# S5 layer with FFN on one Trainium2 core: context scaling and eigenvalue powers on VectorE, accumulating transfers ahead of the pair products

## The chip, the cores and the metric

The kernel runs on one core of a Trainium2 chip, in one launch. The metric is the device time of that launch in microseconds (us); the median of three runs is compared. The core's engines run side by side, each through its own instructions in order, and meet through semaphores: TensorE (PE in the profile, PEld for its weight loads), VectorE (DVE), ScalarE (ACT), GpSimd (POOL) and SyncE (SP), which here only issues transfers. Transfers (DMA) are issued from the queues of SyncE, ScalarE and GpSimd; the ones that add onto their destination are issued from GpSimd.

## The reference

One layer (depth 1) of a hybrid backbone with a bidirectional S5 mixer, over 1024 latent tokens and 256 context tokens of width 1024, all in float32. Cut to what matters here:

```python
def s5_direction(u_ctx, u_lat, lam_re, lam_im, log_step, b_re, b_im, c_re, c_im):
    lam = lax.complex(lam_re, lam_im)
    lam_bar = jnp.exp(lam * jnp.exp(log_step)[:, None])
    b_bar = ((lam_bar - 1.0) / lam)[..., None] * lax.complex(b_re, b_im)
    c_mat = lax.complex(c_re, c_im)
    def run(u, h0):
        bu = jnp.einsum('lgh,gnh->lgn', u, b_bar)
        bu = bu.at[0].add(lam_bar * h0)
        a = jnp.broadcast_to(lam_bar, bu.shape)
        _, h = lax.associative_scan(_linear_combine, (a, bu), axis=0)
        return jnp.einsum('lgn,ghn->lgh', h, c_mat).real, h[-1]
    y_c, h_c = run(u_ctx, jnp.zeros(lam_bar.shape, lam_bar.dtype))
    y_l, _ = run(u_lat, h_c)
    return y_c, y_l

h_l = modulate(rms_norm(x, norm_mix), m_l[0], m_l[1])      # latent tokens, scale and shift from silu(c)
h_c = modulate(rms_norm(ctx, norm_mix), m_c[0], m_c[1])    # context tokens, from silu(c_ctx)
y_c, y_l = s5_mixer(h_c, h_l, ...)                         # both directions, then d_skip, GELU and a GLU
x = x + m_l[2] * y_l
x = x + m_l[5] * swiglu(modulate(rms_norm(x, norm_ffn), m_l[3], m_l[4]), w1, w3, w2)
return rms_norm(x, norm_final)
```

There are 64 groups of 16 channels with 64 complex states each. The context's final state starts the latent scan; the output is the latent stream.

## The kernel before, in words

Eight consecutive tokens form a chunk, so there are 32 context chunks and 128 latent ones. `U` (128 partitions: 8 tokens by 16 channels) holds, for each of the 64 groups, 160 columns: `Xc` the first 32 (context), `X` the other 128 (latent). A *block* `b` is eight groups; there are 8 blocks, and 16 steps `hb` go through 8 blocks by 2 directions. `bd(hb)` gives block and direction: from step 4 on, block `hb // 2` and direction `hb % 2`.

The kernel first computes the eigenvalues' exponentials on VectorE (to about 28 us), then runs the loop over `hb` (L698 to L755), then a scan over chunks on VectorE (`scan`, L839), beside which GpSimd, TensorE and ScalarE work through a written-out list (`PROG1`), and after it `PROG2`, the GLU and the FFN.

What the loop does for one step, and on which engine:

- `sums(hb)`: TensorE multiplies the block's columns of `U` by the weights `Win`, and ScalarE copies the results into the state arrays `STQ` (L590 for direction 0, L592 and L593 for direction 1). Two PSUM buffers `pv` turn, and ScalarE frees them.
- `bl_make(n)`: two products of 128x1024 that make the weights of step `n`, into the buffers `bls(n)`: on GpSimd for the steps in `PMUL` (6, 8, 10, 13 among them), on VectorE for the others (7, 9, 11, 12, 14, 15).
- `bl_sum(n)`: the sum of the two products. For `n` of 4 to 15 it is an accumulating transfer of 512 KB, issued from GpSimd's queue (L433); for `n` above 15 it does nothing.
- `bl_tr(n)`: TensorE transposes the summed weights, ScalarE copies them to `Win` (L446) and copies one more piece (`bb_copy`, L451).
- `pair(n)`: four products and sums of 128x256 that combine neighbouring latent chunks of step `n`, on GpSimd for the steps in `PPAIR` (3, 5, 7, 8, 9, 11, 12, 13, 15), else on VectorE. `ctx_tree` does the like for the context chunks, on VectorE.
- the latent inputs are scaled by the row statistics (`rs_lat`, VectorE) and then by the modulation (`u_act`, ScalarE, L497). The context inputs of block `b` are scaled by `u_ctx(b)`: one product and one sum over 128x256 on GpSimd, with the columns `cols`, which `mix_cols` copies from PSUM to SBUF. `UCTX` (L685) puts blocks 4, 5, 6 and 7 at steps 6, 7, 9 and 11.
- `pw_mul` makes powers of the eigenvalues: four products and sums on GpSimd, called once in step 3 (one power, 128x128 and 128x64 elements) and twice in step 4 (two powers, then one).
- `power8`, `powers` and `pw_full` prepare further powers; `mix_scale`, `mix_sel` and `mix_cols` turn the modulation rows into columns, for groups 0 to 31 ahead of the loop and for 32 to 63 in step 4.

Within a step the order of the source sets each engine's order: `sums(hb)`, `bl_tr(hb+2)`, `rs_lat`, `u_act`, `u_ctx`, `pair(hb-1)`, `ctx_tree`, `bl_sum(hb+5)`, `bl_make(hb+6)`, `pw_mul`. So in step 9 GpSimd has `u_ctx(6)`, `pair(8)` and then the issue of transfer 14; in step 10 `pair(9)` and then the issue of transfer 15.

From step 9 SyncE's queue holds the load of the C columns (`cs_load(0)`, L651), whose buffer is the one that transfer 13 reads, and then, from step 10, the 256 KB loads of the modulation weights (`ada_load`, L520), which write over buffers of the loop. ScalarE changes the sign of part of the C columns in step 11 (`cs_sign(0)`, L655).

The vector engines' elementwise operations all go through the helper `tt` (L77), so lines of the profile are told apart by tiles: `ru` is `U`, `ra` holds the states and the powers, `lta`, `ltb`, `lbt`, `tq` are PSUM banks that VectorE uses for its second operands, `c` and `rxc` hold the weight products, `r` holds `cols` and other small arrays. `colp` are 128 columns of `ltb` that hold modulation columns in PSUM; `u_lat` reads them for blocks 0 and 1 alone.

Of the kernel before, what the change touches and what calls it, by code (L numbers as in the profile page):

```python
# [24 lines left out]
G = 64  # L25
# [17 lines left out]
def s5_ffn_kernel(tc, a, out):  # L43
    nc = tc.nc
    V, S, E, PE, SY = nc.vector, nc.scalar, nc.gpsimd, nc.tensor, nc.sync
    ctx = ExitStack()
    with ctx:
        ctx.enter_context(tc.manual_schedule())
        sb = ctx.enter_context(tc.tile_pool(name="sb", bufs=1))
        def region(tag, kb, dt=F32):  # L50
            return sb.tile([P, int(kb * 256)], dt, tag=tag, name=tag)

        def view(reg, kb, shape, parts=P):
            off = int(round(kb * 256))
            n = int(np.prod(shape))
            v = reg[:parts, off:off + n]
            if len(shape) > 1:
                names = "abcdef"[:len(shape)]
                v = v.rearrange(f"p ({' '.join(names)}) -> p {' '.join(names)}",
                                **{k: d for k, d in zip(names, shape)})  # L60
            return v
# [3 lines left out]
        RA = region("ra", 80.5)  # L65
# [5 lines left out]
        def bc(ap, axis, n):  # L71
            sh = list(ap.shape)
            sh.insert(axis, n)
            return ap.unsqueeze(axis).to_broadcast(sh)

        def tt(o, x, y, op, eng=V):
            eng.tensor_tensor(out=o, in0=x, in1=y, op=op)  # L77
# [10 lines left out]
        MUL, ADD, SUB = OP.mult, OP.add, OP.subtract  # L88
# [10 lines left out]
        ident, blk, sel = (cpk[:, HC + i * P:HC + (i + 1) * P] for i in range(3))  # L99
# [36 lines left out]
        LTb = pA.tile([P, 512], F32, tag="r1", name="ltb")  # L136
        lbt = pA.tile([P, 512], F32, tag="r4", name="lbt")
# [15 lines left out]
        X, Xc = U[:, :, 32:160], U[:, :, 0:32]  # L153
# [41 lines left out]
        def ada1(h, *ks):  # L195
            for k in ks:
                for b in range(2):
                    i = 2 * b + h
                    PE.matmul(prow[32 * i:32 * i + 2], scs[:, k], stage[h][k][:, b], start=k == 0, stop=k == 7, tile_position=(0, 32 * i))
# [79 lines left out]
        rsp, rcp, colp = LTb[:, 256:384], LTb[:, 128:160], LTb[:, 384:512].rearrange("p (b g) -> p b g", b=2)  # L279
# [61 lines left out]
        def pw_mul(o, x, y):  # L341

            m = x.shape[1]
            a_, b_ = (view(RA, kb, [m, 2, G]) for kb in (42, 43))
            yr, yi = (bc(bc(y[:, i], 1, 2), 1, m) for i in range(2))
            tt(a_, x, yr, MUL, E)
            tt(b_, x[:, :, ::-1], yi, MUL, E)
            tt(o[:, :, 0], a_[:, :, 0], b_[:, :, 0], SUB, E)
            tt(o[:, :, 1], a_[:, :, 1], b_[:, :, 1], ADD, E)

        LH = view(RXc, 0, [2, 3, G])
        SQ = [LS[:, 0], view(RXa, 7.25, [3, G]), LH[:, 0], LH[:, 1], LS[:, 1]]
# [1 line left out]
        def power8():  # L354

            pt = pv2()[:, 0, 0:128].rearrange("p (r q d e) -> p r q d e", r=2, q=8, d=2)
            for gp in range(2):
                for d in range(2):
                    sl = slice(64 * d, 64 * d + 64)
                    PE.matmul(pt[64 * gp:64 * gp + 64, :, :, d], ident[:, sl],  # L360
                              PW[:, 7].rearrange("p r (q e t) -> p r q e t", q=8, t=2)[:, :, :, :, gp], start=True, stop=True)
            pt = pt.rearrange("p r q d e -> p r (q d e)")
            S.copy(SQ[0][:, 0::2], pt)
            S.activation(SQ[0][:, 1], pt[:, 1], AF.Copy, scale=-1.0)
            S.copy(LQ[0], SQ[0])
# [36 lines left out]
        def bls(hb):  # L402
            return BL1[hb % 5], BL2[hb % 3]
# [26 lines left out]
        def bl_sum(hb):  # L430

            if 4 <= hb < 16:
                E.dma_start(bls(hb)[0], bls(hb)[1], accum_op=ADD)  # L433
            elif hb < 4:
                tt(bls(hb)[0], bls(hb)[0], bls(hb)[1], ADD, E)

        def bl_tr(hb, copy=True):
            b, d = bd(hb)
            t1 = bls(hb)[0]
            pt, w_ = pv2(), Win[hb % 3]  # L440
            for j in range(2):
                for i in range(4):
                    PE.transpose(pt[:, j, P * i:P * i + P], t1[:, 4 * j + i].rearrange("p s h -> p (s h)"), ident)
            if not copy:
                return pt, w_
            S.copy(w_.rearrange("p j i n -> p (j i n)"), pt.rearrange("p j n -> p (j n)"))  # L446
            bb_copy(hb)
# [5 lines left out]
        r4, mx = view(RA, 74, [4, P]), view(RA, 76, [2, 2, 32])  # L453

        def mix_rows():
            S.copy(r4, prow.rearrange("p (m n) -> p m n", m=4))

        def mix_turn():
            for m in range(4):
                PE.transpose(prow[:, P * m:P * m + P], r4[:, m], ident)  # L460
# [11 lines left out]

        def mix_sel(h):

            PE.matmul(colp[:, :, 32 * h:32 * h + 32], sel, mx[:, 0], start=True, stop=True)
            PE.matmul(pcol, sel, mx, start=True, stop=True)

        def mix_cols(h, eng=V):
# [5 lines left out]

        def u_ctx(b):
            gs = slice(8 * b, 8 * b + 8)
            tt(Xc[:, gs], Xc[:, gs], bc(cols[:, 1, 1, gs], 2, 32), MUL, E)
            tt(Xc[:, gs], Xc[:, gs], bc(cols[:, 1, 0, gs], 2, 32), ADD, E)

# [87 lines left out]
        def sums(hb):  # L577
            b, d = bd(hb)
            for j in range(2):
                w, pv = Win[hb % 3][:, j], pv2()  # L580
                for ri in range(2):
                    for i in range(4):
                        c0 = 160 * (i // 2)
                        PE.matmul(pv[64 * (i % 2):64 * (i % 2) + 64, ri, c0:c0 + 160], w[:, i, 64 * ri:64 * ri + 64],  # L584
                                  U[:, 8 * b + 4 * j + i], start=True, stop=True)
                pv = pv[:, :, 0:320].rearrange("p r (e c) -> p c r e", e=2)
                e = 8 * (b % 2) + 4 * d + 2 * j
                st = STQ[b // 2][:, :, :, e:e + 2]
                if d == 0:
                    S.copy(st, pv)  # L590
                else:
                    S.copy(st[:, 159:31:-1], pv[:, 32:160])  # L592
                    S.copy(st[:, 31::-1], pv[:, 0:32])  # L593
# [104 lines left out]
        for hb in range(16):  # L698
            sums(hb)
            ada1(1, *ADA1.get(hb, ()))  # L700
            if hb == 0:
                power8()
            if hb == 3:
                mix_rows()
            for n in BLTR.get(hb, (hb + 2,)):
                if n < 16:
                    bl_tr(n)
            if hb == 3:
                mix_turn()
            if hb == 4:  # L710
                mix_scale(1)
                mix_sel(1)
            if hb in RSL:
                rs_lat(RSL[hb])
            if hb == 4:
                mix_cols(1)
                tq = pA.tile([P, 512], F32, tag="r3", name="tq")
                LQ += [t[:, o_:o_ + 192].rearrange("p (r e) -> p r e", e=G) for t, o_ in ((tq, 0), (tq, 192), (LTb, 256))]
            if hb == 0:
                tt(Xc[:, 16:], ctxT[:, 16:], bc(rcp, 1, G - 16), MUL)  # L720
            if hb == 1:
                powers(0)
            if hb == 2:
                powers(1)
                SY.dma_start(BXY[:, 1], a["bxy"][:, 3])
            if hb in UACT:
                u_act(*UACT[hb])
            if hb in UCTX:
                u_ctx(UCTX[hb])
            if hb >= 1:  # L730
                pair(hb - 1, E if hb - 1 in PPAIR else V)
            if hb == 5:
                powers(2, 3)
            for a_ in CTREE.get(hb, ()):
                ctx_tree(*a_)
            if hb + 6 in (7, 9, 11, 12, 14, 15):
                lb_psum(hb + 6)
            bl_sum(hb + 5)
            bl_make(hb + 6)
            if hb == 3:  # L740
                pw_mul(PW[:, 2:3], PW[:, 0:1], PW[:, 1])
                tt(KD.rearrange("p q g h -> p (q g) h"), bc(pat, 1, 8), bc(dcol, 2, HC), MUL, E)
            if hb == 4:
                pw_mul(PW[:, 4:6], PW[:, 0:2], PW[:, 3])
                pw_mul(PW[:, 6:7], PW[:, 2:3], PW[:, 3])
            if hb in (6, 8):
                pw_full(hb // 2 - 3)
            if hb == 9:
                cs_load(0)
            if hb == 11:  # L750
                V.tensor_copy(LQ[4], SQ[4])
                cs_sign(0)
            for _ in range(CLAT.get(hb, 0)):
                CL0.pop(0)()
            ada_load(ADA2.get(hb, 0))  # L755
# [752 lines left out]
        for f in list(PAIRS) + [NFT - 2]:  # L1508
# [6 lines left out]
            if f in PAIRS:  # L1515
                U = [("U", f + 1, j) for j in range(7)]
                n = 4 if f == NPL else 1
# [172 lines left out]
        for i, (kind, ft, j) in enumerate(seq):  # L1690
# [12 lines left out]
            if kind == "U":  # L1703
# [4 lines left out]
                if (ft, j) in LAST:  # L1708
                    k, h = LAST[ft, j]
# [63 lines left out]
```

## Time and profile before

| what | us |
|---|---|
| median of 3 runs | 1023.65 |
| lowest and highest run | 1022.72, 1023.95 |
| the profiled execution's own time | 1024.33 |
| its span, first to last instruction | 1022.5 |
| TensorE busy in the span | 962.6 (94%) |
| VectorE busy | 785.6 (77%) |
| GpSimd busy | 762.7 (75%) |
| ScalarE busy | 438.5 (43%) |
| mean granted TensorE clock | 0.987 |

The span begins with the first instruction and all times of rows are counted from there. A row of the timeline has start and duration in us, engine, line, operation, output tile from input tiles, shape and count, and in brackets the idle time ahead of it with what ended it; rows of like instructions in a row are merged. In rows of waits, the engine and line on the left waited for the one on the right: total us, number of times, longest. Rows of DMA issues give the size and the us from issue to landing.

### The profile page before, as it was taken

The numbers are of one execution on the slowest core, as the hardware profiler recorded it, in microseconds if no ns is written. First come the engines' busy times: TensorE is split into PE (matmuls) and PEld (weight loads), VectorE is DVE, ScalarE is ACT, GpSimd is POOL, SyncE is SP. The second block draws the span as 40 slices with busy tenths as digits, with TensorE's granted clock in tenths as the row PEclk, the third lists the DMA queues.
The fourth block names the chain that finished last, engine by engine and source line by source line (L and its number), as shares of the span: only waits on it lengthen the run. The fifth ranks groups of instructions, "written<-read, shape, count | busy, mean of one in ns | idle before, by whom it ended". The sixth has DMA issues, their size and how long they took to land. (4 is left out here: it accounts for less than half of the span.)

```text
span 1022.5 us, 18552 instructions
## 1 busy us (share of the span) xinstructions
PE 962.6 (94%) x6988; PEld 774.2 (76%) x6988; DVE 785.6 (77%) x1642; ACT 438.5 (43%) x858; POOL 762.7 (75%) x590
## 2 busy tenths in 40 slices
PE   5987798868999999999999999999999999999996
PEld 1466523658999988778888888888888888888885
DVE  7989799994365778788968768585958778686977
ACT  5477622324353663533334343424333343324337
POOL 5799999991591457879686877778686877777664
PEclk9999999998999999999999999999999999999998
DMA  9765997222622021011212011121212111121205
GB/s 318 292 132 96 276 350 243 91 73 57 235 80 86 2 104 62 21 42 42 83 41 73 32 52 61 43 73 52 73 42 81 41 40 56 45 70 52 72 21 165
DMA packets 48546, 98.96 MB, mean 97 GB/s; under 512 B 4284, under 2 KB 18876, under 8 KB 47176
## 3 DMA queue, kind: packets, MB, share of 16 engines
q1 hardware_dynamic: 43272, 86.64, 25.3%
q0 software_dynamic: 2016, 7.34, 3.8%
q10 hardware_dynamic: 3168, 3.79, 1.1%
q8 instruction: 55, 0.90, 0.4%
q14 instruction: 35, 0.29, 0.1%
HBM read 84.25 MB, written 6.17 MB: 88 GB/s over the span
## 5 line engine op out<-in xcount | busy, mean ns | idle before, releaser
L77 POOL TENSOR_TENSOR c<-rxc,c 128x512 fp32r<-128x512 f32 x128 | 166.6, 1316 | 53.5 <-ACT c L1227 52.7
L1287 PE MATMUL ut<-ra,c 128*128 128x512 f32 x400 | 155.7, 389 | 1.2 <-DVE ra L77 1.2
L1286 PE MATMUL ut<-ra,c 128*128 128x512 f32 x400 | 155.7, 389 | 0.2 <-ACT ra L1227 0.2
L1288 PE MATMUL ut<-ra,c 128*128 128x512 f32 x400 | 155.6, 389 | 0.0
L1227 ACT CAST c<-rxc 128x512 fp32r<-128x512 f32 x128 | 79.1, 622 | 146.8 <-PE xt L1581 53.3
L1581 PE MATMUL xt<-c,c 128*128 128x512 f32 x540 | 129.7, 389 | 0.0
L1581 PEld LDWEIGHTS xt<-c,c 128*128 128x128 f32 x540 | 101.4, 188 | 21.0
L77 DVE TENSOR_TENSOR ru<-ru,xt 128x1024 f32<-128x1024 f32 x90 | 106.8, 1213 | 8.6 <-PE xt L1581 6.6
L77 DVE TENSOR_TENSOR ru<-ut,ru 128x512 f32<-128x512 f32 x98 | 67.1, 686 | 43.1 <-PE ut L1288 37.7
L1287 PEld LDWEIGHTS ut<-ra,c 128*128 128x128 f32 x400 | 75.1, 188 | 17.1 <-POOL rxc L77 1.5
L1286 PEld LDWEIGHTS ut<-ra,c 128*128 128x128 f32 x400 | 75.1, 188 | 16.1 <-ACT ra L1227 0.6
L1288 PEld LDWEIGHTS ut<-ra,c 128*128 128x128 f32 x400 | 75.1, 188 | 15.5
L77 POOL TENSOR_TENSOR c<-rw,c 128x512 fp32r<-128x512 f32 (+1 forms) x29 | 42.5, 1465 | 38.8 <-ACT c L1227 38.2
L1286 PE MATMUL ut<-c,c 128*128 128x512 f32 x160 | 62.3, 389 | 0.8 <-DVE rxa L77 0.8
L77 POOL TENSOR_TENSOR c<-ru,c 128x512 fp32r<-128x512 f32 (+1 forms) x39 | 55.5, 1422 | 10.1 <-ACT c L1227 5.7
L77 POOL TENSOR_TENSOR rxc<-rxc 128x512 f32<-128x512 f32 x40 | 61.5, 1536 | 1.6
L1288 PE MATMUL ut<-c,c 128*128 128x512 f32 x160 | 62.3, 389 | 0.0
L1287 PE MATMUL ut<-c,c 128*128 128x512 f32 x160 | 62.3, 389 | 0.0
L1581 PE MATMUL ut<-c,c 128*128 128x512 f32 x216 | 51.9, 389 | 0.0
L584 PE MATMUL pv<-ru,c 128*64 128x160 f32 x512 | 43.7, 312 | 7.3 <-POOL ru L77 2.6
L77 DVE TENSOR_TENSOR pe<-pe,ru 128x256 f32<-128x256 f32 x64 | 27.4, 428 | 29.5 <-ACT pe L1127 17.4
L77 DVE TENSOR_TENSOR ru<-ru,ut 128x512 f32<-128x512 f32 x76 | 47.2, 678 | 0.7 <-ACT ru L1635 0.5
(449 smaller groups left out, 2576.0 us busy)
## 6 DMA issues: line engine op xcount, KB each, us to landing
c<-in_ada_w SPq DMA_DIRECT2D x46, 256.0 KB
rxc<-in_w SPq DMA_DIRECT2D x38, 256.0 KB
rxc<-in_w SPq DMA_DIRECT2D x19, 512.0 KB
ru<-in_w SPq DMA_DIRECT2D x11, 512.0 KB
rw<-in_w SPq DMA_DIRECT2D x11, 512.0 KB
ra<-in_ada_w SPq DMA_DIRECT2D x10, 512.0 KB
ra<-in_ada_w SPq DMA_DIRECT2D x18, 256.0 KB
ru<-in_xT SPq DMA_DIRECT2D x4, 1024.0 KB
```

The lines of the kernel that those rows point to most:

```text
L77: eng.tensor_tensor(out=o, in0=x, in1=y, op=op)
L584: PE.matmul(pv[64 * (i % 2):64 * (i % 2) + 64, ri, c0:c0 + 160], w[:, i, 64 * ri:64 * ri + 64], U[:, 8 * b + 4 * j + i], start=True, stop= ...
L1227: S.copy(o[0], x)
L1286: PE.matmul(pu, wh, bh, start=start, stop=False)
L1287: PE.matmul(pu, wh, bl, start=False, stop=False)
L1288: PE.matmul(pu, wl, bh, start=False, stop=stop)
L1581: PE.matmul(pd, w[:, cs_], b, start=j in (1, 2, 4) and n == 0, stop=n == 2, skip_group_check=j not in (1, 2, 4))
```

## The change

Three parts, all in the loop and what it calls:

1. `pw_mul` runs on VectorE. It first copies the factor `y` into a PSUM bank (`yc`, in `lbt`), and its two temporaries are a piece of `ltb` (PSUM) and one of `ra`.
2. `u_ctx` for blocks 4 to 7 runs on VectorE and reads its columns from `colp` in PSUM. For that `mix_sel(1)` writes the context columns (`mx[:, 1]`) of groups 32 to 63 into `colp`, where before it wrote the latent ones.
3. In steps 9 and 10 the issue of the accumulating transfer, `bl_sum(14)` and `bl_sum(15)`, stands ahead of `pair(8)` and `pair(9)` in place of behind them.

```diff
         def pw_mul(o, x, y):
             m = x.shape[1]
-            a_, b_ = (view(RA, kb, [m, 2, G]) for kb in (42, 43))
-            yr, yi = (bc(bc(y[:, i], 1, 2), 1, m) for i in range(2))
-            tt(a_, x, yr, MUL, E)
-            tt(b_, x[:, :, ::-1], yi, MUL, E)
-            tt(o[:, :, 0], a_[:, :, 0], b_[:, :, 0], SUB, E)
-            tt(o[:, :, 1], a_[:, :, 1], b_[:, :, 1], ADD, E)
+            a_, b_ = (t[:, :128 * m].rearrange("p (m r n) -> p m r n", m=m, r=2) for t in (LTb, view(RA, 42, [256])))
+            yc = lbt[:, 256:384].rearrange("p (r n) -> p r n", r=2)
+            V.tensor_copy(yc, y)
+            yr, yi = (bc(bc(yc[:, i], 1, 2), 1, m) for i in range(2))
+            tt(a_, x, yr, MUL)
+            tt(b_, x[:, :, ::-1], yi, MUL)
+            tt(o[:, :, 0], a_[:, :, 0], b_[:, :, 0], SUB)
+            tt(o[:, :, 1], a_[:, :, 1], b_[:, :, 1], ADD)
...
-            PE.matmul(colp[:, :, 32 * h:32 * h + 32], sel, mx[:, 0], start=True, stop=True)
+            PE.matmul(colp[:, :, 32 * h:32 * h + 32], sel, mx[:, h], start=True, stop=True)
...
         def u_ctx(b):
             gs = slice(8 * b, 8 * b + 8)
+            if b > 3:
+                tt(Xc[:, gs], Xc[:, gs], bc(colp[:, 1, gs], 2, 32), MUL)
+                tt(Xc[:, gs], Xc[:, gs], bc(colp[:, 0, gs], 2, 32), ADD)
+                return
             tt(Xc[:, gs], Xc[:, gs], bc(cols[:, 1, 1, gs], 2, 32), MUL, E)
             tt(Xc[:, gs], Xc[:, gs], bc(cols[:, 1, 0, gs], 2, 32), ADD, E)
...
             if hb in UCTX:
                 u_ctx(UCTX[hb])
+            if hb > 8:
+                bl_sum(hb + 5)
             if hb >= 1:
                 pair(hb - 1, E if hb - 1 in PPAIR else V)
...
-            bl_sum(hb + 5)
+            if hb < 9:
+                bl_sum(hb + 5)
             bl_make(hb + 6)
```

## The prediction

> **What bounds the kernel now.** I read three views in this order: the stretches of the span, the waits inside the loop, then the timelines of the engines. In the stretches (length, then busy time of each engine with its instruction count, the granted clock, the DMA share and GB/s) the reader is to see which engine has no room:
>
> ```profile
> 68.69:111.37 42.68, 33.72 (x337) 26.12 (x338) 39.77 (x107) 33.20 (x71) 41.58 (x59) 0.96 0.58 121
> 111.37:128.72 17.35, 14.34 (x141) 8.58 (x143) 10.14 (x41) 10.13 (x24) 14.82 (x17) 0.92 1.02 315
> 128.72:228.60 99.88, 83.13 (x1512) 48.08 (x1504) 97.75 (x508) 26.44 (x55) 96.84 (x66) 0.96 0.58 191
> 228.60:267.50 38.90, 35.76 (x985) 33.32 (x985) 18.00 (x28) 14.62 (x21) 10.76 (x11) 0.91 0.40 123
> 267.50:1022.50 755.00, 744.05 (x3695) 632.30 (x3692) 561.61 (x790) 316.73 (x621) 550.60 (x402) 1.00 0.19 61
> ```
>
> The columns are TensorE, its weight loads, VectorE, ScalarE, GpSimd. After 228.60 TensorE is all but full (744.05 of 755.00 us), so what follows has a fixed length. The scan before it keeps VectorE busy for 97.75 of 99.88 us: fixed too. What can move is the scan's start at 128.72. In the loop ahead of it VectorE (39.77 of 42.68 us) and GpSimd (41.58) are both full up to 111.37, and only then does VectorE idle. Who it waits for (rows of waits), and what waits for the scan (timeline of TensorE):
>
> ```profile
> DVE ltb L77 <- ACT ra L593: 5.4, 2, 4.7
> ...
> DVE ltb L77 <- ACT ra L590: 1.2, 1, 1.2
> ...
> 228.72 0.70 PE L922 MATMUL pe<-c,ra 64*64 64x128 f32 x4 [4.71 <-DVE ra L77]
> ```
>
> VectorE waits 5.4 + 1.2 = 6.6 us, always for ScalarE's copies of the last state sums (steps 13 to 15). TensorE had idled 4.71 us when the scan's end released it at 228.72, so a later scan makes the run later by as much, and work beside the scan may slip by up to 4.7 us unseen.
>
> **The prices on VectorE.** The prologue has the same complex product (a copy and four products), and the loop the same in-place pair against a PSUM operand; starts are subtracted:
>
> ```profile
> 21.73 0.28 DVE L316 COPY ltb<-ra 128x128 f32<-128x128 f32 x1
> ...
> 22.96 0.43 DVE L77 TENSOR_TENSOR lta<-ra,ltb 128x256 f32<-128x256 f32 x1
> ...
> 24.15 0.28 DVE L319 COPY ltb<-ra 128x128 f32<-128x128 f32 x1
> ...
> 25.78 0.43 DVE L77 TENSOR_TENSOR lta<-ra,ltb 128x256 f32<-128x256 f32 x1
> ...
> 58.92 0.41 DVE L77 TENSOR_TENSOR ra<-ra,ltb 128x256 f32<-128x256 f32 x1
> 59.36 0.42 DVE L77 TENSOR_TENSOR ra<-ra,lbt 128x256 f32<-128x256 f32 x1
> 59.70 1.21 DVE L77 TENSOR_TENSOR ru<-ru,ltb 128x1024 f32<-128x1024 f32 x1
> ```
>
> A product of one power costs 22.96 - 21.73 = 1.23 us, of two 25.78 - 24.15 = 1.63 us. Step 3 adds one of the first, step 4 one of each: 2 x 1.23 + 1.63 = 4.1 us. A context block (two passes over 128x256) costs 59.70 - 58.92 = 0.78 us; four make 3.1 us, in steps 6, 7, 9 and 11. VectorE gains 7.2 us of work, all ahead of 111.37, where it has no gap to take it. I take these prices as they are: the loop's rows ran beside a full GpSimd already.
>
> **What GpSimd loses, and what it then waits for.**
>
> ```profile
> 69.63 1.83 POOL L77 TENSOR_TENSOR ra<-ra 128x128 f32<-128x128 f32 x4
> ...
> 79.12 4.25 POOL L77 TENSOR_TENSOR ra<-ra 128x256 f32<-128x256 f32 x8
> ...
> 83.93 1.60 POOL L77 TENSOR_TENSOR ru<-ru,r 128x256 f32<-128x256 f32 x2
> ...
> 90.37 0.88 POOL L433 DMA_DIRECT2D c<-c  x1
> ...
> 97.92 0.87 POOL L433 DMA_DIRECT2D c<-rxc  x1
> ...
> 102.83 0.86 POOL L433 DMA_DIRECT2D c<-c  x1
> 103.44 1.57 POOL L77 TENSOR_TENSOR rxc<-ra,r 128x256 f32<-128x256 f32 x2
> ...
> 106.45 0.86 POOL L433 DMA_DIRECT2D c<-c  x1
> ...
> 108.62 1.29 POOL L77 TENSOR_TENSOR rxc<-ra,r 128x256 f32<-128x256 f32 x2
> ...
> 123.37 1.56 POOL L77 TENSOR_TENSOR rxc<-ra,r 128x256 f32<-128x256 f32 x2
> 124.62 1.80 POOL L77 TENSOR_TENSOR ra<-ra,rxc 128x256 f32<-128x256 f32 x2
> ...
> 129.06 2.03 POOL L77 TENSOR_TENSOR rw<-rxc,rxa 128x1024 f32<-128x1024 f32 x1 [2.64 <-DMA c<-rw]
> ```
>
> GpSimd is freed of 1.83 + 4.25 + 4 x 1.60 = 12.5 us. But its DMA issues need VectorE's products (`bl_make`), and those now end later:
>
> ```profile
> 81.23 1.21 DVE L77 TENSOR_TENSOR ru<-ru,ltb 128x1024 f32<-128x1024 f32 x1
> ...
> 88.48 0.42 DVE L77 TENSOR_TENSOR ltb<-ra,lta 128x256 f32<-128x256 f32 x1
> ...
> 103.10 0.42 DVE L77 TENSOR_TENSOR ltb<-ra,lta 128x256 f32<-128x256 f32 x1
> ...
> 128.72 0.29 DVE L77 TENSOR_TENSOR ltb<-ra,lta 128x128 f32<-128x128 f32 x1
> ...
> 129.12 0.29 DVE L77 TENSOR_TENSOR ra<-ltb,ra 128x128 f32<-128x128 f32 x1
> ```
>
> The product of block 12 ends at 88.48 now; with 4.1 + 0.78 more at 93.4. GpSimd, early by then, stands idle until that. From the issue of transfer 12 to that of 13 it took 97.92 - 90.37 = 7.55 us, so 13 goes at 100.9 instead of 97.92. The product of block 15 ends at 103.10 now, then at 103.10 + 4.1 + 3 x 0.78 = 109.5. So transfer 15, meant to start ahead, starts at 109.5 where it started at 106.45; transfer 14 at 102.8 as before, since its product also ends some 6 us later. And whoever stands behind the issue of 15 waits with it: pair(9), which before ran ahead of it (103.44 to 106.45, 3.01 us). This is the cost of the moved issue; it would be nothing if VectorE's product were there first. Edits without a cost: `mix_sel` has the same matmuls, and the columns that it now fills for groups 32 to 63 had no reader. The TensorE issue behind it in step 4 is 1.2 us later, under its own later wait.
>
> **Three ways to the scan's start.**
> *VectorE alone:* 7.2 more work less 6.6 of waits that it then no longer meets: +0.6 us.
> *GpSimd:* from 109.5, issue 103.44 - 102.83 = 0.61, pair(9) 3.01, and from pair(11) to the end of pair(15) 124.62 + 1.80 - 108.62 = 17.80: it ends at 130.9. The scan's third instruction (129.12) adds into columns that pair(15) writes, so it moves to 130.9: +1.8 us.
> *TensorE and ScalarE* (timelines of TensorE, ScalarE and SyncE, then rows of DMA issues for transfers 13, 14, 15):
>
> ```profile
> 85.59 3.78 PE L584 MATMUL pv<-ru,c 128*64 128x160 f32 x32 [2.62 <-POOL ru L77]
> ...
> 110.82 1.06 PE L443 MATMUL pv<-r,c 128*128 128x128 f32 x8 [1.23 <-DMA c<-c]
> ...
> 115.50 1.07 PE L443 MATMUL pv<-r,c 128*128 128x128 f32 x8 [1.15 <-ACT ra L593]
> ...
> 108.42 0.83 ACT L655 ACTIVATE rxc<-rxc 128x768 f32<-128x768 f32 x1
> ...
> 103.05 0.33 SPq L651 DMA_DIRECT2D rxc<-in_cxy  x1
> ...
> c<-rxc POOLq DMA_DIRECT2D x1, 512.0 KB, 5.1
> ...
> c<-c POOLq DMA_DIRECT2D x1, 512.0 KB, 7.9
> ...
> c<-c POOLq DMA_DIRECT2D x1, 512.0 KB, 8.9
> ```
>
> The sums of block 4 start at 85.59, released by GpSimd; VectorE gives that block after step 6's row at 81.23: 81.23 + 4.1 + 1.21 + 0.78 = 87.3, 1.7 us late. Transfers 13, 14 and 15 land after 5.1, 7.9 and 8.9 us. The load of the C columns (103.05) waits for transfer 13 and so goes at 100.9 + 5.1 = 106.0; of the same size, it lands by 111.1 by the same row, and ScalarE, whose sign change at 108.42 stands ahead of the next state copies, waits until then: 2.7 us late. The transposes of block 14 lose the 1.23 us that they waited for their transfer, so about +1.5 us is left, which the last copies carry on to VectorE. The transposes of block 15 need transfer 15: bounds 109.5 + 5.1 = 114.6 and 109.5 + 8.9 = 118.4 (115.50 now, so nothing or +2.9). The weight loads that slowed 14 and 15 also start some 3 us later and still meet 15, but 14 is out of the way; I take the middle, 116.5 (+1.0), and keep both ends.
>
> The largest decides: +1.8 us, and with the hand-overs about **+1.9 us**. The profiled execution took 1024.33 us (span 1022.5 and 1.8 around it), so 1026.2; the median of the runs shown, 1023.65, lies 0.7 below it: **1025.5 us**.
>
> The Trainium skill ("PSUM — Partial Sum Buffer", Engine vs sequencer instructions) calls the GpSimd queue strictly first in, first out. Before shows GpSimd waiting for a transfer at 129.06 with all behind it, but no long wait of an issue; by the rule pair(9) waits as above, without it pair(15) would end 3.0 us sooner and the third way would decide, at +1.5. The skill ("DMA: Bandwidth & Descriptors", Issuing engines are not separate DMA queues) has all transfers share the same engines; the rows of 7.9 and 8.9 us agree with it. By it transfer 15 is slowed further by the loads, the first rival.
>
> **Rivals.**
> *Transfer 15 is late (slower).* If the 256 KB loads hold it for 8.9 us again, block 15 is transposed at 118.4 and the scan moves by 2.9 us: 1026.6. It decides from a landing at 117.7 on. For it: a share of 1.02 from 111.37. Against: transfer 14 no longer shares that time. Chance 0.28.
> *GpSimd's backlog.* Its next product (129.06) waits for another transfer, issued behind pair(13), so it comes about 4.3 us later. Past the 4.71 us of cover the stage after the scan would wait: about +4, 1027.6. Chance 0.07.
> *VectorE alone.* If GpSimd and the transfers keep up: +0.6, 1024.3. Chance 0.18.
> *GpSimd was the pace (faster).* Freed of 12.5 us it would bring the last sums forward, and VectorE, if it did the added work at half the rows' price (3.6 us), would save 6.6 - 3.6 = 3.0: 1020.6. It needs an added cost under 4.6 us, which the rows speak against; with what may come later, 0.05.
> *It doesn't do what it says:* the transfers start no earlier. That is part of the forecast.
>
> **Numbers.** Forecast 0.42. A difference of 0.2% (2.05 us) is about what a measurement of this kernel can tell from no change, and the forecast lies just under it: 0.32 of its chance within, 0.10 beyond. Within: 0.32 + 0.18 = 0.50. Slower: 0.10 + 0.28 + 0.07 = 0.45. Faster: 0.05. The range goes from VectorE alone, less the 0.9 us by which the lowest run lies under the median (1023.3), to the backlog (1027.6).
>
> **What would show it.** Right: GpSimd idle ahead of its issues in steps 6 to 10, transfer 15 issued near 109.5 with pair(9) behind it, no wait of VectorE for ScalarE near 111, pair(15) ending near 131, scan start near 130.6, every later stage as long as before. Wrong: VectorE's block products ending less than 5 us later, transfer 15 issued before 106.45, or a scan start under 129.

## The result, and the profile after

| kernel | median us (runs) | ratio to before, 95% interval | profiled execution, its span |
|---|---|---|---|
| before | 1023.11 (6) | | 1024.33, 1022.5 |
| after | 1029.28 (6) | 1.0061, 1.0051 to 1.0072 | 1028.65, 1026.8 |

The change makes the kernel slower by about 6 us. The forecast was 1025.5 us with a range of 1023.3 to 1027.6, so the loss is about three times the forecast one, on the side that the first two rivals had named. Lines of kernel.py that stand behind the edit have moved down by 2 to 9.

The stretches of the span, as before (length, busy time and instructions of TensorE, its weight loads, VectorE, ScalarE and GpSimd, granted clock, DMA share, GB/s); the first one ends at the same place of VectorE's work as the first of before:

```profile
67.76:118.66 50.90, 39.05 (x372) 29.84 (x372) 46.73 (x130) 37.17 (x81) 33.79 (x40) 0.93 0.60 132
118.66:133.53 14.87, 12.11 (x104) 7.35 (x108) 10.12 (x41) 6.08 (x13) 12.66 (x15) 0.80 0.88 265
133.53:233.40 99.87, 84.85 (x1512) 47.81 (x1504) 97.77 (x508) 26.54 (x55) 96.37 (x66) 0.96 0.58 190
233.40:272.30 38.90, 33.53 (x983) 31.25 (x984) 16.95 (x28) 14.73 (x21) 14.44 (x14) 0.96 0.39 127
272.30:1026.80 754.50, 744.09 (x3695) 632.38 (x3693) 559.52 (x790) 316.68 (x621) 547.58 (x399) 1.00 0.19 61
```

The scan and the two stages behind it last 99.87, 38.90 and 754.50 us, where they lasted 99.88, 38.90 and 755.00. All of the loss lies ahead of the scan's start, which moved from 128.72 to 133.53. VectorE is still almost full in the first stretch (46.73 of 50.90 us). GpSimd, which was busy for nearly the whole first stretch of before (41.58 of 42.68 us), is now busy for 33.79 of 50.90.

The prologue of two executions differs by up to about a microsecond (the place named next came at 66.4 to 67.6 us over all the kernels below), so I count from a fixed place in the loop: the second VectorE product for the weights of step 9, the only one of its kind that waits over 3 us for a transfer. The timeline of VectorE, before and then after:

```profile
67.55 1.22 DVE L77 TENSOR_TENSOR c<-c,lbt 128x1024 f32<-128x1024 f32 x1 [3.25 <-DMA c<-c]
...
100.83 2.35 DVE L77 TENSOR_TENSOR c<-c,lbt 128x1024 f32<-128x1024 f32 x2 [0.20 <-ACT ra L590]
```

```profile
66.50 1.22 DVE L77 TENSOR_TENSOR c<-c,lbt 128x1024 f32<-128x1024 f32 x1 [3.27 <-DMA c<-c]
...
107.21 2.35 DVE L77 TENSOR_TENSOR c<-c,lbt 128x1024 f32<-128x1024 f32 x2 [0.20 <-PE pv L445]
...
126.08 0.43 DVE L77 TENSOR_TENSOR ltb<-ra,lta 128x256 f32<-128x256 f32 x1 [3.41 <-ACT ra L596]
...
128.31 0.43 DVE L77 TENSOR_TENSOR ltb<-ra,lta 128x256 f32<-128x256 f32 x1 [0.68 <-ACT ra L599]
...
133.53 0.29 DVE L77 TENSOR_TENSOR ltb<-ra,lta 128x128 f32<-128x128 f32 x1
```

From that place the scan starts 133.53 - 66.50 = 67.03 us on, where it was 128.72 - 67.55 = 61.17: **5.9 us later**, close to the 6.2 us between the medians. VectorE still idles 3.41 + 0.68 us for the last state sums, so it isn't the pace. The chain that it waits for is read from the timelines of GpSimd, TensorE and SyncE and the DMA issues of the changed kernel (the last number of an issue is the us to its landing); the row at 103.48 alone is from before, whose loads start there:

```profile
93.68 0.86 POOL L435 DMA_DIRECT2D c<-c  x1 [7.25 <-DVE ru L77]
...
110.14 0.87 POOL L435 DMA_DIRECT2D c<-c  x1 [3.34 <-DVE ru L77]
110.75 1.58 POOL L77 TENSOR_TENSOR rxc<-ra,r 128x256 f32<-128x256 f32 x2
...
129.76 1.80 POOL L77 TENSOR_TENSOR ra<-ra,rxc 128x256 f32<-128x256 f32 x2
```

```profile
112.11 1.09 PE L445 MATMUL pv<-r,c 128*128 128x128 f32 x8 [1.18 <-ACT ra L596]
...
120.07 1.31 PE L445 MATMUL pv<-r,c 128*128 128x128 f32 x8 [4.40 <-DMA c<-c]
...
233.55 3.63 PE L931 MATMUL pe<-c,ra 64*64 64x128 f32 x56 [4.29 <-DVE ra L77]
```

```profile
103.48 22.19 SPq L520 DMA_DIRECT2D c<-in_ada_w  x22
```

```profile
107.07 23.29 SPq L526 DMA_DIRECT2D c<-in_ada_w  x22
```

```profile
c<-c POOLq DMA_DIRECT2D x1, 512.0 KB, 9.8
```

The reader is to see one chain in the changed kernel. VectorE's product for step 15 ends at 107.21 + 2.35 = 109.56; GpSimd, idle for 3.34 us, issues transfer 15 at 110.14; the weight loads of SyncE have been running since 107.07; the transfer takes 9.8 us; the transposes of block 15 wait 4.40 us for it until 120.07, and the state sums, VectorE and the scan follow. In before, the same transfer landed 38.90 + 8.9 = 47.8 us from the fixed place and the transposes ran at 47.95, released by ScalarE: it was not waited for, but it had next to no room, so whatever it loses at its issue is paid at once. (The other 0.2 us of the scan's delay come behind the transposes.)

### The profile page after: what moved, and what is told of

It reads as the page before. It is cut to its first block, busy times and chain, and to the rows that moved or that the text cites. A ratio compares the mean times of both kernels' runs of the same rounds, so it can differ in the third digit from the quotient of the medians.

```text
span 1026.8 us, 18551 instructions
## 1 busy us (share of the span) xinstructions
PE 965.3 (94%) x6988; PEld 774.5 (75%) x6988; DVE 789.0 (77%) x1665; ACT 438.4 (43%) x858; POOL 753.1 (73%) x570
## 5 line engine op out<-in xcount | busy, mean ns | idle before, releaser
L590 PE MATMUL pv<-ru,c 128*64 128x160 f32 x512 | 45.8, 323 | 5.0 <-ACT rxa L390 1.8
```

## The experiments

In the expectations, "theory" is mostly this chain: VectorE's added work delays the product of step 15, so transfer 15 is issued later, lands later beside the weight loads, and holds TensorE, ScalarE and the scan. The table has all runs; columns two to six are us from the fixed place above, worked out from each trace in the same way, with the landing in us from the issue.

| kernel | product 15 ends | transfer 15 issued | lands after | transposes of 15 | scan starts | ratio to before, 95% interval |
|---|---|---|---|---|---|---|
| before | 35.63 | 38.90 | 8.9 | 47.95 | 61.17 | |
| after | 43.06 | 43.64 | 9.8 | 53.57 | 67.03 | 1.0061, 1.0051 to 1.0072 |
| a_parts12 | 43.02 | 43.58 | 9.9 | 53.60 | 66.81 | 1.0067, 1.0042 to 1.0092 |
| a_part1 | 39.84 | 41.92 | 10.0 | 52.02 | 65.23 | 1.0039, 1.0027 to 1.0052 |
| a_part2 | 38.59 | 39.15 | 9.5 | 48.81 | 62.43 | 1.0003, 0.9994 to 1.0012 |
| a_part3 | 35.63 | 36.21 | 9.0 | 47.49 | 60.73 | 0.9997, 0.9981 to 1.0013 |
| b_held | 43.03 | 43.62 | 4.5 | 50.19 | 63.44 | 1.0107, 1.0091 to 1.0123 |
| b_held12 | 42.52 | 43.07 | 4.5 | 50.69 | 63.94 | 1.0067, 1.0053 to 1.0081 |
| b_prod12 | 40.34 | 40.93 | 9.6 | 50.63 | 64.72 | 1.0042, 1.0027 to 1.0057 |
| b_p3held | 36.02 | 36.60 | 6.9 | 47.19 | 60.43 | 1.0001, 0.9987 to 1.0015 |
| c_p3u | 35.65 | 36.24 | 8.8 | 45.87 | 60.35 | 0.9986, 0.9978 to 0.9995 |
| c_p3u13 | 35.93 | 36.52 | 8.1 | 47.65 | 59.45 | 0.9968, 0.9956 to 0.9979 |
| c_u | 35.66 | 38.80 | 8.9 | 47.88 | 60.21 | 0.9991, 0.9982 to 0.9999 |

### The parts, one by one

**Parts 1 and 2 without part 3** (against the changed kernel; the issue of transfers 14 and 15 back behind the pair products):

```diff
-            if hb > 8:
-                bl_sum(hb + 5)
             if hb >= 1:
                 pair(hb - 1, E if hb - 1 in PPAIR else V)
...
-            if hb < 9:
-                bl_sum(hb + 5)
+            bl_sum(hb + 5)
```

> Parts 1 and 2 of the change without part 3: the issues of transfers 14 and 15 stay behind pair(8) and pair(9). Theory (VectorE's added work makes the product of step 15 late, and with it transfer 15, whose landing lets the last transposes and so the scan begin): the issue of transfer 15 still waits for VectorE, so it goes near 110 us as in the changed kernel, lands near 120, scan start near 133.5; time as the changed kernel, 6 us above before (within 1). Rival (the moved issue is to blame, since pair(9) and all of GpSimd's work stands behind it): pair(15) ends 3 us sooner and the run is 2 to 4 us faster than the changed kernel.

The timeline of GpSimd in this kernel:

```profile
109.98 0.88 POOL L435 DMA_DIRECT2D c<-c  x1 [1.62 <-DVE ru L77]
```

With pair(9) ahead of it, GpSimd still stands idle for 1.62 us until VectorE's product lets it issue transfer 15. Issue, landing and scan are those of the changed kernel within about 0.2 us, and so is the ratio within its interval (its six runs spread from 1024.29 to 1034.03 us): moving the issue ahead gains nothing where the product is late, and costs nothing either.

**Part 1 alone** (the power products; this and the next two against the kernel before):

```diff
         def pw_mul(o, x, y):
...
+            V.tensor_copy(yc, y)
+            yr, yi = (bc(bc(yc[:, i], 1, 2), 1, m) for i in range(2))
+            tt(a_, x, yr, MUL)
...
```

> Part 1 alone (the power products on VectorE). Theory: the product of step 15 ends about 4.7 us later than before, the issue of transfer 15 is then held by GpSimd's own work (near 109, 1.2 us ahead of the changed kernel), and the scan starts about 1.5 us sooner than in the changed kernel: 4 to 5 us above before. Rival (GpSimd was the pace, and the power products leave it): at or below before.

Product 15 is 39.84 - 35.63 = 4.2 us later, as the prediction priced it (4.7 was expected here), transfer 15 3.0 and the scan 4.1; the median is 3.7 us above that of before (1026.06 against 1022.40). The timelines of GpSimd, ScalarE and TensorE show that transfer 15 isn't the only way by which VectorE's lateness gets there:

```profile
92.41 0.88 POOL L435 DMA_DIRECT2D c<-c  x1 [5.11 <-DVE ltb L77]
...
108.47 0.87 POOL L435 DMA_DIRECT2D c<-c  x1
```

```profile
112.36 0.84 ACT L657 ACTIVATE rxc<-rxc 128x768 f32<-128x768 f32 x1 [1.62 <-DMA rxc<-in_cxy]
```

```profile
113.86 1.09 PE L445 MATMUL pv<-r,c 128*128 128x128 f32 x8 [2.03 <-ACT ra L592]
...
118.57 1.06 PE L445 MATMUL pv<-r,c 128*128 128x128 f32 x8 [1.16 <-ACT ra L595]
```

GpSimd idles 5.11 us ahead of the issue of transfer 12, so transfer 13 goes later too, and the load of the C columns behind it; ScalarE's sign change waits 1.62 us for that load, the transposes of block 14 for ScalarE, and those of block 15, at 118.57, for ScalarE again. Transfer 15 goes when GpSimd gets to it, 2.1 us after the product, and lands at 108.47 + 10.0 = 118.5. Two chains end here within 0.1 us of each other, so this run doesn't show the landing as the cause.

**Part 2 alone** (the context blocks and the columns that they read):

```diff
         def u_ctx(b):
             gs = slice(8 * b, 8 * b + 8)
+            if b > 3:
+                tt(Xc[:, gs], Xc[:, gs], bc(colp[:, 1, gs], 2, 32), MUL)
+                tt(Xc[:, gs], Xc[:, gs], bc(colp[:, 0, gs], 2, 32), ADD)
+                return
```

> Part 2 alone (context blocks 4 to 7 on VectorE). Theory: VectorE's 2.7 us ahead of the product of step 15 are covered by the time by which GpSimd reached the issue of transfer 15 later than that product (106.45 against 103.1): transfer 15 goes near 106.4 as before, and the time is that of before within 1 us. Rival (each microsecond on VectorE counts): 2.5 to 3.5 us above before.

Product 15 is 3.0 us later, but the issue only 0.25. In before, GpSimd issued transfer 15 38.90 - 35.63 = 3.3 us after the product was ready; of that, a GpSimd that stands ready needs 0.6 between product and issue (the hand-over), so the room is 2.7, and part 2 uses up just that. In its trace the scan starts 1.3 us later, with a landing of 9.5 us; the medians show no clear difference (1023.16 against 1022.40). With both parts the product is far beyond the room: 4.2 + 3.0 = 7.2 us late (7.4 measured), and 4.7 at the issue.

**Part 3 alone** (the moved issues, `bl_sum` as in the diff of the change):

```diff
+            if hb > 8:
+                bl_sum(hb + 5)
             if hb >= 1:
                 pair(hb - 1, E if hb - 1 in PPAIR else V)
```

> Part 3 alone (the issues of transfers 14 and 15 ahead of pair(8) and pair(9)). Theory: VectorE's products are there in time, so transfer 14 goes near 100.1 in place of 102.8 and transfer 15 near 103.7 in place of 106.45, both ahead of most of the weight loads; the transposes of step 14 no longer wait (1.2 us) and the time is 1 us below before. Rival (the moved issue holds up GpSimd): 2 to 3 us above before.

The median is 0.7 us lower, and the interval takes in no change. The timelines of VectorE and TensorE show why there is so little to gain:

```profile
114.55 0.43 DVE L77 TENSOR_TENSOR ltb<-ra,lta 128x256 f32<-128x256 f32 x1 [4.31 <-ACT ra L593]
```

```profile
113.91 1.09 PE L443 MATMUL pv<-r,c 128*128 128x128 f32 x8 [1.06 <-ACT ra L593]
```

Transfer 15 now goes 2.7 us sooner, and no transposes wait for a transfer any more (those of block 14 waited 1.23 us in before); TensorE waits for ScalarE's state copies, and VectorE with it.

### Is it the landing, and is it the loads?

**The weight loads held back** (against the changed kernel). `stg` lists the buffers that the loads write; its first entries now lie in transfer 15's source, so SyncE's first load waits for that transfer, and all loads behind it in the queue:

```diff
-        stg = [view(r, kb + 2 * i, [512]) for r, kb, n in ((RC[2], 8, 4), (RC[1], 4, 6), (RC[3], 4, 2), (RC[0], 8, 4), (RC[1], 0, 2))
+        stg = [view(r, kb + 2 * i, [512]) for r, kb, n in ((RC[1], 12, 2), (RC[2], 8, 4), (RC[1], 4, 4), (RC[3], 4, 2), (RC[0], 8, 4), (RC[1], 0, 2))
...
-        stg = (stg + sl_ + (sx_ + stg[:4] + sl_) * 2 + (sx_ + stg[:4]) * 3)[:64]
+        stg = (stg + sl_ + (sx_ + stg[2:6] + sl_) * 2 + (sx_ + stg[2:6]) * 3)[:64]
```

> The changed kernel with the weight loads on SyncE held back until transfer 15 has landed (the first load writes over transfer 15's source buffer, so it must wait). Theory (transfer 15 is late and is slowed by the loads): with no loads beside it, it lands 4.6 to 5.8 us after its issue near 110.1, so at 114.7 to 116 in place of 120; the transposes of block 15 stop waiting for it, the scan starts when pair(15) ends, near 131.6, 2.3 us sooner than in the changed kernel: about 1027, still 3 to 4 us above before. Rival A (VectorE's and ScalarE's own chain is what is late, the landing only happens to end with it): scan start unchanged, 1029. Rival B (the landing time has nothing to do with the loads): landing after 9 to 10 us again, 1029.

The DMA issue of transfer 15, then the timelines of SyncE, VectorE and TensorE:

```profile
c<-c POOLq DMA_DIRECT2D x1, 512.0 KB, 4.5
```

```profile
115.39 22.94 SPq L526 DMA_DIRECT2D c<-in_ada_w  x22
```

```profile
132.18 0.29 DVE L77 TENSOR_TENSOR ra<-ltb,ra 128x128 f32<-128x128 f32 x1 [1.14 <-POOL ra L77]
```

```profile
117.29 1.09 PE L445 MATMUL pv<-r,c 128*128 128x128 f32 x8 [1.07 <-ACT ra L599]
...
139.66 1.87 PE L537 MATMUL pm<-c,r 128*2 128x512 f32 x2 [4.88 <-DMA c<-in_ada_w]
...
238.59 4.74 PE L931 MATMUL pe<-c,ra 64*64 64x128 f32 x128 [0.67 <-ACT ru L1006]
```

The first half of the expectation came as written; rival B falls, and rival A is left with a part. Issued at the same place of the loop, the same transfer takes 4.5 us without the loads and 9.8 with them; no one waits for it any more, the scan starts 3.6 us sooner, and its third instruction now waits 1.14 us for pair(15) on GpSimd. This run parts the loss in two: the late landing is worth 3.6 of the 5.9 us, and the 63.44 - 61.17 = 2.3 us that are left come by ScalarE's and TensorE's chain (the transposes of block 15 now wait for ScalarE, 50.19 - 47.95 = 2.2 us later than in before). That second part is read from the trace; no run takes it away. The Trainium skill ("DMA: Bandwidth & Descriptors", Issuing engines are not separate DMA queues) has the transfers of all queues interleave on the same engines; the two durations agree.

The total did not follow: 1033.58 us, 4.3 above the changed kernel. The loads start at 115.39 in place of 107.07, 7.7 us later from the fixed place (at 67.10 here), and TensorE now waits for them (4.88 us near 139). I had put that under the cover of 4.7 us at the scan's end, though 7.7 is more; the stage behind the scan starts at 238.59, not when the scan ends: 171.49 us from the fixed place, against 167.05 in the changed kernel, 4.4 us later. Held back this far, the loads lose more behind the scan than the transfer gains ahead of it.

**The same without part 3** (its edit, too, against the changed kernel):

```diff
-        stg = [view(r, kb + 2 * i, [512]) for r, kb, n in ((RC[2], 8, 4), (RC[1], 4, 6), (RC[3], 4, 2), (RC[0], 8, 4), (RC[1], 0, 2))
+        stg = [view(r, kb + 2 * i, [512]) for r, kb, n in ((RC[1], 12, 2), (RC[2], 8, 4), (RC[1], 4, 4), (RC[3], 4, 2), (RC[0], 8, 4), (RC[1], 0, 2))
...
-            if hb > 8:
-                bl_sum(hb + 5)
```

> Parts 1 and 2 of the change without the moved issues, and the weight loads held back in the same way. Theory: as with the loads held in the changed kernel, but pair(9) runs ahead of the waiting issue, so pair(15) ends some 3 us sooner and no longer holds the scan: 1 to 1.5 us below the changed kernel with held loads, near 1025.5. If the waiting issue at the head of GpSimd's queue costs nothing there: the same as the changed kernel with held loads.

VectorE no longer waits for GpSimd, so the head of GpSimd's queue was what held pair(15). But the scan itself starts 0.5 us later than with part 3, as do the transposes of block 15 (50.69 against 50.19), which are now what it follows; without the wait of 1.14 us it is 0.7 us ahead from its third instruction on. The median is 4.2 us under that of the run before it, 3 more than expected, and nearly all of that lies later, at the late loads: the stage behind the scan starts 2.9 us sooner. What shortened it there was not tried.

**The products of step 12 on GpSimd**, which idles 7.25 us ahead of transfer 12 in the changed kernel:

```diff
-        PMUL = (1, 3, 5, 6, 8, 10, 13)
+        PMUL = (1, 3, 5, 6, 8, 10, 12, 13)
...
-            if hb + 6 in (7, 9, 11, 12, 14, 15):
+            if hb + 6 in (7, 9, 11, 14, 15):
```

> The changed kernel with the two weight products of step 12 on GpSimd in place of VectorE (GpSimd idles 7.25 us ahead of that transfer). Theory (VectorE's lateness, carried on by transfer 15's issue): VectorE is freed of 2.7 us, the product of block 15 ends and transfer 15 goes near 107.3 instead of 110.1, and the scan starts 2.5 to 3.7 us sooner: 1025.5 to 1026.8. Rival (GpSimd's work is what counts): GpSimd gets about 7 us of products and is as late as before or later, 1029 or above.

VectorE's product 15 and the issue behind it come 2.7 us sooner, and the scan 2.3: 1027.44 us, a little above what was expected, with an interval that still touches that of the changed kernel. In the trace, giving VectorE room moves the scan, while GpSimd with two products more is not later. That is VectorE's lateness, not GpSimd's work.

### From there to a faster kernel

**Part 3 alone with the loads held** (against the kernel before):

```diff
+            if hb > 8:
+                bl_sum(hb + 5)
...
-        stg = (stg + sl_ + (sx_ + stg[:4] + sl_) * 2 + (sx_ + stg[:4]) * 3)[:64]
+        stg = (stg + sl_ + (sx_ + stg[2:6] + sl_) * 2 + (sx_ + stg[2:6]) * 3)[:64]
```

> Part 3 alone on the kernel before, with the weight loads held back until transfer 15 has landed. Theory: transfer 15 no longer waits for the loads, but in this kernel no one waits for it any more, so the gain is that of part 3 alone, 0.5 to 1.5 us below before (1021 to 1022); the loads some 8 us later stay under the 4.7 us that TensorE idles at the scan's end. If the later loads come out from under that cover: 1 to 4 us above before.

No gain: the scan starts 0.3 us sooner than with part 3 alone, and the later loads put the start of the stage behind it back from 160.73 to 165.33 us, from the fixed place.

**Part 3 and the scaling of block 7 on VectorE** (this and the next two against the kernel before). With part 3 alone, ScalarE's state copies of steps 13 and 14 stand behind four activations that scale the latent inputs. This kernel takes the latter to VectorE in steps 12 and 13:

```diff
-        def u_act(b, n0, n1):
+        def u_act(b, n0, n1, vec=False):
             for g in range(8 * b + n0, 8 * b + n1):
+                if vec:
+                    ts(X[:, g], X[:, g], cols[:, 0, 1, g:g + 1], MUL, cols[:, 0, 0, g:g + 1], ADD)
+                    continue
...
-                u_act(*UACT[hb])
+                u_act(*UACT[hb], hb in (12, 13,))
```

> Part 3 alone on the kernel before, and the latent scaling of block 7 (four activations on ScalarE, 1.65 us, in step 12 and again in step 13) on VectorE. In the run of part 3 alone no transfer is waited for any more, and what sets the scan's start is the chain of TensorE and ScalarE in steps 13 to 15, where the state copies of sums stand behind these activations; VectorE idles 4.31 + 1.14 + 0.69 us for it. Theory: each of the two takes about 1.3 us out of that chain (a copy waits until TensorE's 1.31 us are done in any case), VectorE has room for some 2 x 1.0 us more: scan start 2 to 2.7 us sooner than with part 3 alone, 1019 to 1020 (ratio to before near 0.997). Rival (the state copies are not what the scan waits for, or VectorE's added work is): no gain, 1021.5 to 1023.

Half of the forecast gain on before came, 0.9986, but next to nothing against part 3 alone (1021.52 us against 1021.66), and the scan starts 0.4 us sooner in place of 2 to 2.7: that is the rival, VectorE's added work. The instructions of this line, then the timelines of VectorE and of GpSimd beside it:

```profile
L86 DVE TENSOR_SCALAR ru<-ru,r x8: 472/712/2059, 105.4 to 112.5; 128x128 f32<-128x128 f32 x8
```

```profile
105.37 2.52 DVE L86 TENSOR_SCALAR ru<-ru,r 128x128 f32<-128x128 f32 x4
...
109.26 3.93 DVE L86 TENSOR_SCALAR ru<-ru,r 128x128 f32<-128x128 f32 x4
```

```profile
110.51 2.02 POOL L77 TENSOR_TENSOR c<-rxc,rxa 128x1024 f32<-128x1024 f32 x1
```

TensorE's and ScalarE's chain did shorten (the transposes of block 15 come 1.6 us sooner than with part 3 alone), but one scaling (shortest, median and longest in ns) took 712 ns in the median, where I had put 250, and the longest, 2059 ns from 110.6 on, ran while GpSimd's product of 2.02 us did. VectorE, with 2.52 + 3.93 = 6.45 us more in place of 2, waits for no one and has become the pace. The Trainium skill ("SBUF — State Buffer", Who interferes with whom) has VectorE's `tensor_scalar` with operands in SBUF able to block against GpSimd for a whole instruction; the 2059 ns beside the 2.02 us agree with it, and VectorE's operations around them, which have an operand in PSUM, keep their 0.41 to 0.42 us.

**The same in step 13 alone:**

```diff
-                u_act(*UACT[hb])
+                u_act(*UACT[hb], hb in (13,))
```

> The same with the activations of step 13 alone on VectorE. Theory: half of that gain, 1.0 to 1.4 us below part 3 alone, about 1020.4. Rival: 1021.5 to 1023.

The timelines of VectorE and of TensorE in this kernel:

```profile
114.83 0.43 DVE L77 TENSOR_TENSOR ltb<-ra,lta 128x256 f32<-128x256 f32 x1 [2.22 <-ACT ra L596]
```

```profile
226.00 5.03 PE L928 MATMUL pe<-c,ra 64*64 64x128 f32 x128 [0.76 <-DVE ra L77]
```

VectorE still waits 2.22 us for ScalarE, and the scan starts 1.3 us sooner than with part 3 alone: as the theory has it. At 1019.23 us it is the fastest kernel here, 0.32% under before (0.21 to 0.44%; its runs spread from 1017.22 to 1023.19). More than the scan's start is in that: behind the scan the profiled execution (1017.44 us) lasts 1015.7 - 226.00 = 789.7 us, where before it was 1022.5 - 228.72 = 793.8. The stretch of 20 us behind the scan's end, in before and then in this kernel:

```profile
228.72:248.72 20.00, 17.50 (x607) 16.31 (x608) 8.24 (x16) 7.97 (x12) 6.00 (x9) 0.84 0.09 28
```

```profile
226.00:246.00 20.00, 17.57 (x650) 16.25 (x654) 10.00 (x20) 10.59 (x16) 10.05 (x14) 1.00 0.14 42
```

TensorE waited 0.76 us for the scan here and 4.71 in before, and then got a clock of 1.00 where it had 0.84. That is not the whole of it: with the loads held in the changed kernel it had 1.00 too, and the run behind the start of that stage lasted 792.8 us. Why TensorE was later ahead of the scan's end here was not tried.

**The same scaling on the kernel before, without part 3:**

```diff
-                u_act(*UACT[hb])
+                u_act(*UACT[hb], hb in (12, 13,))
```

> The kernel before, without part 3, with the activations of steps 12 and 13 on VectorE. Theory: the chain of TensorE and ScalarE is a little later here, since the transposes of block 14 wait 1.23 us for their transfer; the gain is the 1.3 us of step 13 and at most that of step 12, 1 to 2.5 us below before (1020 to 1021.3). If the transposes of block 15 now meet their transfer, which landed near 115.4 in before, it is only 1 us.

The timeline of TensorE:

```profile
109.79 1.06 PE L443 MATMUL pv<-r,c 128*128 128x128 f32 x8 [1.25 <-DMA c<-c]
...
114.45 1.07 PE L443 MATMUL pv<-r,c 128*128 128x128 f32 x8 [1.13 <-DMA c<-c]
```

The transposes of block 15 do meet their transfer (1.13 us), and the gain is the small one, 1.3 us of the medians (1021.47 against 1022.78). VectorE is the pace here too, so this pair of runs says nothing on what part 3 is worth.

## Why the prediction was wrong

- **What bounds, and what can move.** Right: the stages behind the scan's start kept their lengths within 0.5 us, and the whole loss is the later start.
- **The prices on VectorE.** Part 1 was priced at 4.1 and measured 4.2 us. Part 2 was priced at 3 x 0.78 = 2.3 ahead of product 15 and measured 3.0. Together 6.4 against 7.4: 1.0 us short, of which 0.5 is a longer wait of `mix_cols` for TensorE (1.31 us, 0.80 in before). "VectorE alone" was rightly not the pace.
- **GpSimd's way.** GpSimd did idle ahead of its issues (7.25 and 3.34 us), pair(9) did stand behind the issue of transfer 15, and pair(15) ended at 129.76 + 1.80 = 131.56. On the count of before, whose prologue took 1.05 us longer, that is 132.6, where 130.9 was forecast: the 1.7 us between them are those of the later issue. The Trainium skill ("PSUM — Partial Sum Buffer", Engine vs sequencer instructions) has the queues of ScalarE, VectorE and GpSimd strictly first in, first out; the trace agrees, with pair(9) at 110.75, right behind the issue at 110.14. But this way does not decide: the scan's third instruction comes at 133.94. It decides once the landing is out of the way, as the held loads showed with 1.14 us.
- **TensorE's and ScalarE's way: the step that failed.** It is the term for transfer 15, where the prediction put the landing between 114.6 and 118.4 and took "the middle, 116.5 (+1.0)". It landed at 110.14 + 9.8 = 119.9, which is 121.0 on the count of before, 4.5 us behind that middle. Three parts make that up. The issue came at 43.64 from the fixed place, 4.7 us later than before in place of 3.05: 1.0 for VectorE's prices and 0.6 between the end of the product and the issue. And the transfer took 9.8 us in place of the 7.0 that the middle stood for. Its reason, that transfer 14 would be out of the way, was no reason: 14 had landed at 103.15 + 5.8 = 109.0, and the loads alone doubled the time of 15 (9.8 against 4.5 us). The rest of this way, by transfer 13 and the C columns, was put at "about +1.5"; the held loads leave 2.3.
- **The rival "Transfer 15 is late"** had the mechanism. It named 117.7 as the landing from which it decides; by its own rows that is 115.50 + 1.8 = 117.3. It was priced at the 8.9 us of before and the issue of 109.5, so at +2.9; the same chain with 43.64 and 9.8 gives 4.7 + 0.9 = 5.6 at the transposes, and 5.6 was measured there (53.57 - 47.95). It had a chance of 0.28. The 8.9 us of before were no upper bound: that transfer, too, was issued 3.0 us after the first load (106.45 against 103.48), and the one of the changed kernel, 3.1 us after it, took 0.9 us longer. Why is open.
- **"GpSimd was the pace"** falls: GpSimd has 12.5 us less to do and the run is longer; with two products more on GpSimd it is shorter.
- **"GpSimd's backlog"** did not act: the product that it names came 5.9 us later (133.92 against 129.06, from the fixed place), with the scan, and TensorE still waited 4.29 us for the scan's end at 233.55.

## What to carry to other kernels

Before work goes to another engine, look for the transfer or the semaphore that waits for that engine's next results, and measure the room between the result and its use (here 3.3 us, 2.7 without the hand-over): 3.0 us of added work cost little, 7.4 were paid as 4.7 at the issue. Follow every transfer of that queue, not the last alone. A transfer's duration holds only for what ran beside it: here one took 9.8 us inside a burst of loads and 4.5 without it. Holding the loads back only pays if their own users have as much room. Freed time on an engine is worth nothing until one finds who was waiting for it.

## What the runs showed of the hardware

- The accumulating transfer of 512 KB took 4.5 us with the 256 KB loads held back until it had landed (6.9 in the kernel with part 3, where the load of the C columns was issued at the same time), 8.8 to 10.0 us when it was issued after those loads had begun, and 8.1 when they began 0.7 us behind it.
- An issue on GpSimd that waited for VectorE began 0.55 to 0.59 us after the end of the product of step 15 (in the changed kernel 109.56 to 110.14).
- VectorE's scaling of 128x128 with both scalars from SBUF took from 339 to 2060 ns beside a busy GpSimd, over the three kernels that do it.
- Behind a wait of TensorE of 2.1 to 5.8 us at the scan's end, the clock granted over the next 20 us was 0.83 to 0.92. In three of the four kernels with a wait under 0.8 us it was 1.00; in the fourth, the loads held without part 3, it was 0.91, with a wait of 4.12 us some 12 us earlier. The Trainium skill ("TensorE: Matmul & The Clock Gate", HAM oscillation — how this bites in real kernels) warns of idle gaps over some 3.4 us; these rows agree, though the one wait of 2.1 us went with 0.91 as well.
